# A state-space and gating mixer layer on one core: other buffers for the readout's tables, another split of the state copies, kernels between half blocks

## The chip, the core and the metric

The kernel runs on one NeuronCore of a Trainium2 chip. The metric is the device time of one execution in microseconds (us); the number for a version is the median over its runs. Engines are named as in the profile: PE is TensorE (PEld its weight loads), DVE is VectorE, ACT is ScalarE, POOL is GpSimd, SP is SyncE, whose queue issues every DMA of this kernel.

## What is computed

The reference is one layer over 1024 latent rows of width 1024 (float32). With `h` the layer-normed and modulated input and `p = h @ w_in + b_in` split into `ua, za, ub, vb, zb, ga, gb`:

```python
y_a, _ = _s5_bidir(ua, discs, ssm_c_re[i], ssm_c_im[i], ssm_d[i], ctx_final, True)
ya = _ssm_glu_gate(y_a, za, glu_w[i], glu_b[i])        # gelu(y), half-GLU, * silu(za)
yb = _sgu_branch(ub, vb, zb, ...)                      # gelu(ub) * (W_s v + b) * silu(zb)
out = _merge_out(ya, yb, ga, gb, w_branch_a[i], w_branch_b[i], w_out[i], b_out[i])
x = _layer_norm(DEEPNORM_ALPHA * x + gate[:, None] * out) * ln_g[i] + ln_b[i]
```

`_s5_bidir` is a diagonal linear recurrence over the positions, forward and backward, with 32 groups of 16 channels and 64 complex states a group; its output is read out of the states, with a direct term from the inputs. A context of 256 rows gives the recurrence its first state.

## The kernel before, in words

Tile builds the program: the code gives instructions in program order, each tile takes a free buffer of its pool, and a scheduler lays out, ahead of time and with its own estimate of durations, the order in which every engine's queue runs them; earlier lines have the higher priority. A queue runs strictly in the order it was given. Every large product is done as three float32r products (`mm3`, L75) of high and low halves; the halves of a weight are made on ACT (L72) and DVE (L73) from a staged copy.

**Pools** (L49 to L55): `G`, 27 buffers of 128x1024 float32; `WSP`, 6 of the same size, in which the high and low halves of the weights rotate as three pairs; `RAW`, 3, for the staged weights; `TMP`, 4 of 128x512; `ROW`, 2 of 128x1280; `BIG`, one, which holds the recurrence's states `vst` in the middle of the kernel. Sixteen of the `G` buffers hold the transposed `h` (`hth`, `htl`) until late.

**Recurrence in blocks of 8 positions.** `ua` is written to DRAM (`ud`) and read back in a block layout; `v_in` and `v_out` make the block inputs of all states; `scan` (L604) steps through the 158 blocks on DVE, three small operations a step. Steps 1 to 49 stand ahead of the other branch's projection, 50 to 158 beside it.

**Tables.** `out_powers(b)` (L625), for `b` 0 to 3 (8 groups each), makes on DVE two readout tables `kca` (six operations of 128x1024 for the two directions) and writes them to DRAM (`cad`). `kernels(b, d)` (L634) multiplies them on PE with `bbar` to the short convolution kernels inside a block, and writes these to DRAM (`wd`). These stand (L660 to L673) around two projection blocks, UB+2 and UB+3, each of which `proj` (L551) does as two half blocks of 512 rows, 24 products each; `mid` is called between the two halves.

**Branch B** (L829 to L839): eight times a projection of gate GB+i (48 products) and a product with `w_b` (24), `then_b` on DVE, and the result `mb` (a `G` buffer) to DRAM (`md`). The weights of block 27 (GB+7), `w_b3` and block 12 (the first of ZA) are split in this stage and hold the three pairs of `WSP` at its end.

**Readout** (L768 to L850). `y_tables(b)` loads from DRAM two tables `ca` (512 KB each; `G` for b = 0, `WSP` for the rest), a kernel table `mt` in eight pieces of 64 KB (`RAW`), and the rows of u, `um`, in two halves (`TMP`). `y_states(b)` (L781) copies the states from `vst` to two `G` tiles `z`, in eight copies of 64x512: four on ACT (L790), four on DVE (L792). `y_mm(b)` (L795) does 8 groups on PE, each one product with `mt` and `um` (L801) and two with `ca` and `z` (L803), and the gelu on ACT into `gk` (`ROW`). `y_trans(b)` (L808) transposes `gk` on PE (`pg`, L813) into `gT`. Program order on PE is y_mm 0, y_mm 1, trans 0, y_mm 2, trans 1, y_mm 3, trans 2, trans 3. In program order `y_tables(0)` and `y_states(0)` stand behind branch 6, `y_tables(1)` behind branch 7, and `y_states(b + 1)` and `y_tables(b + 2)` behind `y_mm(b)`.

After that come the projections ZA (`act_into`, L875), the GLU, branch A and the output product, on PE without a break until the tail.

Of the kernel before, what the change touches and what calls it, by code (L numbers as in the profile page):

```python
# [8 lines left out]
F32 = mybir.dt.float32  # L9
F32R = mybir.dt.float32r  # L10
I32 = mybir.dt.int32
AF = mybir.ActivationFunctionType
# [4 lines left out]
T = 8  # L17
# [9 lines left out]
UB, ZB, ZA, GA, GB = 0, 4, 8, 12, 20  # L27
# [8 lines left out]
def mixer_kernel(ctx: ExitStack, tc: tile.TileContext, a, out):  # L36
    nc = tc.nc
    V, S, Pl, PE = nc.vector, nc.scalar, nc.gpsimd, nc.tensor
# [5 lines left out]
    def pool_of(tag, bufs, dshape, ddt=F32):  # L44
        def make(name, shape=dshape, dt=ddt):
            return sb.tile(list(shape), dt, name=name, tag=tag, bufs=bufs)
        return make

    G = pool_of("g", 27, (128, 1024))  # L49
    BIG = pool_of("big", 1, (128, 2 * NSLOT * 32))  # L50
    RAW = pool_of("raw", 3, (128, 1024))
    WSP = pool_of("wsp", 6, (128, 1024), F32R)
    TMP = pool_of("tmp", 4, (128, 512))
    ROW = pool_of("row", 2, (128, 1280))
# [5 lines left out]
    def BANK(name, shape=(128, 512)):  # L60
        return psum.tile(list(shape), F32, name=name, tag="b", bufs=8)

    def dma(o, i):
        nc.sync.dma_start(o, i)
# [190 lines left out]
    ud = dram.tile([4, T, 128, 160], F32, name="ud")  # L255
# [200 lines left out]
    for j in range(2):  # L456
        t = RAW(f"xc{j}")
# [36 lines left out]
    for b in range(4):  # L494
        p = BANK(f"pcu{b}")
# [6 lines left out]
    def outer(dst, tmp, eng, pr, xr, xi, b, d, last):  # L502

        gs = slice(32 * d + 8 * b, 32 * d + 8 * b + 8)
        sh = [128, 8, 8, 16]

        def bc(i, x):
            return (pr[:, :, i, gs].rearrange("p k g -> p g k").unsqueeze(3).to_broadcast(sh),
                    x[:, gs, :].unsqueeze(2).to_broadcast(sh))
        p0, x0 = bc(0, xr)  # L510
        p1, x1 = bc(1, xi)
        eng.tensor_tensor(dst, p0, x0, op=OP.mult)
        eng.tensor_tensor(tmp, p1, x1, op=OP.mult)
        eng.tensor_tensor(dst, dst, tmp, op=last)
# [36 lines left out]
    def proj(blk, evac, ahead=None, mid=None):  # L551

        if ahead is None:
            ahead = 0 if blk == GB + 7 else 2
        wh, wl = weights(f"blk{blk}", ahead)
        for hf in range(2):
            p = BANK(f"pp{blk}{hf}")
            sl = slice(512 * hf, 512 * hf + 512)
            for k in range(8):
                mm3(p, wh[:, k, :], wl[:, k, :], hth[k][:, sl], htl[k][:, sl], k == 0, k == 7)  # L560
            evac(p, sl)
            if mid is not None and hf == 0:
                mid()

    def act_into(blk, fn, dst=None, then=None, ahead=None, mid=None):
        def evac(p, sl):
            t = dst[:, sl] if dst is not None else TMP("act")
            S.activation(t, p, fn, bias=cols[:, C_BLK + blk:C_BLK + blk + 1])
            if then is not None:
                then(t, sl)  # L570
        proj(blk, evac, ahead, mid)
# [4 lines left out]
    vm = [G("vm0")]  # L576
# [48 lines left out]
    def out_powers(b):  # L625
        for d in range(2):
            ca = G(f"kca{b}{d}", (128, 8, 8, 16))
            outer(ca, ROW("katmp", (128, 8, 8, 16)), V, pc, xcr, xci, b, d, OP.subtract)
            dma(cad[b, d], ca.rearrange("p g i h -> p (g i h)"))
            kca[b, d] = ca  # L630
# [3 lines left out]
    def kernels(b, d):  # L634
        if d == 0:
            pks[b] = BANK(f"pk{b}", (128, 2, 256))
        pk = pks[b]
        ca = kca[b, d]
        gg = 32 * d + 8 * b
        for k in range(4):  # L640
            for par in range(2):
                lh = bbar[:, gg + 2 * k:gg + 2 * k + 2, :].rearrange("p g h -> p (g h)")
                o = pk[32 * k:32 * k + 32, par, :]
                g = 2 * k + par
                PE.matmul(o[:, 128 * d:128 * d + 112], lh, ca[:, g, d:d + 7, :].rearrange("p i h -> p (i h)"),
                          start=True, stop=True)
                PE.matmul(o[:, 128 * d + 112:128 * d + 128], lh, xcr[:, gg + g, :], start=True, stop=True)
        if d == 0:
            return
        wk = TMP(f"wk{b}", (128, 2, 240))  # L650
        S.activation(wk[:, :, 0:112], pk[:, :, 128:240], AF.Copy)
        S.activation(wk[:, :, 128:240], pk[:, :, 0:112], AF.Copy)
        dm = TMP(f"dm{b}", (128, 3, 16))
        V.tensor_scalar(dm[:, 2, :], mask, cols[:, C_D + b:C_D + b + 1], None, op0=OP.mult)
        V.tensor_tensor(dm[:, 0:2, :], pk[:, :, 112:128], dm[:, 2, :].unsqueeze(1).to_broadcast([128, 2, 16]), op=OP.add)
        V.tensor_tensor(wk[:, :, 112:128], pk[:, :, 240:256], dm[:, 0:2, :], op=OP.add)
        for g in range(8):
            dma(wd[8 * b + g], wk[16 * g:16 * g + 16, g % 2, :])
# [2 lines left out]
        vm.append(G(f"vm{i}"))  # L661
    out_powers(0)
    out_powers(1)
    act_into(UB + 2, AF.Gelu_apprx_tanh, dst=vm[2])
    kernels(0, 0)
    kernels(0, 1)
    out_powers(2)
    kernels(1, 0)
    kernels(1, 1)
    out_powers(3)  # L670
    act_into(UB + 3, AF.Gelu_apprx_tanh, dst=vm[3], mid=lambda: (kernels(2, 0), kernels(2, 1)))
    kernels(3, 0)
    kernels(3, 1)  # L673

    scan(1, 50)

# [65 lines left out]
    for i in range(2, 4):  # L742
        def then(t, sl):
            V.tensor_tensor(vm[i][:, sl], vm[i][:, sl], t, op=OP.mult)
# [3 lines left out]
    def branch(i, g0, w, y, then):  # L748

        banks = []  # L750

        def evac(p, sl):
            t = TMP("act")
            S.activation(t, p, AF.Sigmoid, bias=cols[:, C_BLK + g0 + i:C_BLK + g0 + i + 1])  # L754
            banks.append((t, sl))
        proj(g0 + i, evac)
        wh, wl = weights(f"{w}{i // 2}")
        cs_ = slice(128 * (i % 2), 128 * (i % 2) + 128)
        for t, sl in banks:
            p = BANK(f"pb{g0 + i}")  # L760
            for k in range(4):
                mm3(p, wh[:, k, cs_], wl[:, k, cs_], y[k][0][:, sl], y[k][1][:, sl], k == 0, k == 3)
            then(t, p, sl)


    cas, mts, ums, zs, gks, gt = {}, {}, {}, {}, {}, []

    def y_tables(b):  # L768
        for d in range(2):
            ca = (G if b == 0 else WSP)(f"ca{b}{d}", (128, 8, 8, 16), F32)  # L770
            dma(ca.rearrange("p g i h -> p (g i h)"), cad[b, d])
            cas[b, d] = ca
        mts[b] = RAW(f"mt{b}", (128, 8, 128))
        for s in range(8):
            dma(mts[b][16 * s:16 * s + 16],
                wd[8 * b:8 * b + 8, :, 16 * (7 - s):16 * (7 - s) + 128].rearrange("g h w -> h g w"))
        ums[b] = [TMP(f"um{b}{h}", (128, 4, 128)) for h in range(2)]
        for h in range(2):
            dma(ums[b][h], ud[b].rearrange("t (h g) c -> (t h) g c", g=8)[:, 4 * h:4 * h + 4, 32:160])

    def y_states(b):  # L781
        for d in range(2):
            zt = G(f"z{b}{d}", (128, 8, 128))
            o = 31 if d == 0 else 33
            for cp in range(2):
                for par in range(2):
                    dst = zt[64 * cp:64 * cp + 64, par:8:2, :]
                    src = vst[64 * par:64 * par + 64, d, o:o + 128, cp, 4 * b:4 * b + 4].rearrange("p c q -> p q c")
                    if par == 0:
                        S.activation(dst, src, AF.Copy)  # L790
                    else:
                        V.tensor_copy(dst, src)  # L792
            zs[b, d] = zt

    def y_mm(b):  # L795
        gks[b] = ROW(f"gk{b}", (128, T, 128))
        for h in range(2):
            p = BANK(f"py{b}{h}", (128, 4, 128))
            for i in range(4):
                g = 4 * h + i  # L800
                PE.matmul(p[:, i, :], ums[b][h][:, i, :], mts[b][:, g, :], start=True, stop=False)  # L801
                for d in range(2):
                    PE.matmul(p[:, i, :], zs[b, d][:, g, :], cas[b, d][:, g].rearrange("p i h -> p (i h)"),  # L803
                              start=False, stop=d == 1)
            S.activation(gks[b][:, :, 64 * h:64 * h + 64].rearrange("p t (g h) -> p g t h", h=16),
                         p.rearrange("p g (t h) -> p g t h", h=16), AF.Gelu_apprx_tanh)
# [23 lines left out]
    for i in range(8):  # L830
        mb = G(f"mb{i}")

        def then_b(t, p, sl):
            V.tensor_tensor(mb[:, sl], t, p, op=OP.mult)
        branch(i, GB, "w_b", yb, then_b)
        dma(md[i], mb)
        if i == 6:
            y_tables(0)
            y_states(0)  # L839

    y_tables(1)
    for b in range(4):
# [44 lines left out]
    for i in range(8):  # L887
# [16 lines left out]
        if i == 4:  # L904
# [3 lines left out]
            for h in range(2):  # L908
                p = BANK(f"pga{h}")
# [141 lines left out]
```

## Time and profile before

| | |
|---|---|
| median of 3 runs (742.08 to 742.7) | 742.08 us |
| the profiled execution | 743.85 us |
| its span, first to last instruction | 742.1 us |
| mean granted TensorE clock | 0.992 |
| PE busy | 710.3 us, 96% |
| DVE, ACT, POOL busy | 465.1, 244.5, 38.5 us |
| readout on PE, from the first `py` product to the first ZA product | 415.84 to 449.00 us |

The profile is one execution. Its span leaves out 1.75 us around the instructions that the execution's own time has. PE's clock is given as a share of the higher of its two levels (2.4 GHz), so 0.5 is the lower (1.2 GHz). Idle time of an engine is listed with what ended it; idle time of an engine that does not hold up the others costs nothing.

### The profile page before, as it was taken

Reading aid. Unit: us, or ns where it says so; the run is one execution under the profiler, and the core shown is the slowest. Engines: PE = TensorE matmul, PEld = TensorE weight load, DVE = VectorE, ACT = ScalarE, POOL = GpSimd, SP = SyncE. Lnnn points to the kernel's source line nnn. Section 1 sums busy time; section 2 is a strip of 40 time slices with the busy share of each in tenths; the row PEclk is TensorE's granted clock in tenths of the full one; section 3 lists DMA queues with packets and bytes.
Section 4 is the critical chain, followed back from the end, with each engine's and each line's share of the span. In section 5 each row is a group of like instructions: output and inputs, shape, how many; then the busy total and the mean of one; then the engine's idle time right before and its main releaser. Section 6 shows DMA issues by size and latency. Waiting matters only on the chain.

```text
span 742.1 us, 10068 instructions
## 1 busy us (share of the span) xinstructions
PE 710.3 (96%) x3924; PEld 587.5 (79%) x3924; DVE 465.1 (63%) x1059; ACT 244.5 (33%) x348; POOL 38.5 (5%) x41
## 2 busy tenths in 40 slices
PE   3889999999999999999999979999999999999995
PEld 1656798887888888888888968888888878888885
DVE  4487963569789585899995535134543334592995
ACT  3357737751105423111121865135111211350000
POOL 1010133000001000000000000000000000000221
PEclk9999999999999999999999999999999999999998
DMA  7950273624411211121216674111353223151441
GB/s 301 346 211 30 57 207 114 192 86 150 134 57 30 76 45 52 57 86 57 85 61 193 189 211 150 50 57 57 133 179 114 86 87 112 58 187 40 157 144 69
DMA packets 40783, 87.27 MB, mean 118 GB/s; under 512 B 8352, under 2 KB 21280, under 8 KB 40736
## 3 DMA queue, kind: packets, MB, share of 16 engines
q1 hardware_dynamic: 40736, 86.63, 34.9%
q8 instruction: 31, 0.51, 0.3%
q14 instruction: 16, 0.13, 0.1%
HBM read 70.92 MB, written 15.70 MB: 117 GB/s over the span
## 4 chain that ended last, share of the span: by engine, by line
PE 87%; DVE 5%; ACT 3%; DMA 2%; issue 1%; SPq 0%; POOL 0%; DVEq 0%; ACTq 0%; POOLq 0%
PE pp L77 13%; PE pp L78 13%; PE pp L79 13%; PE po L947 4%; PE po L946 4%; PE po L945 4%; PE pb L78 4%; PE pb L79 4%; PE pb L77 4%; PE pvb L690 2%; PE pvb L691 2%; PE pvb L692 2%; PE pv L546 2%; PE py L803 2%; PE pu L77 1%; PE pm L206 1%
## 5 line engine op out<-in xcount | busy, mean ns | idle before, releaser
L77 PE MATMUL pp<-hh,h_blk 128*128 128x512 f32 x448 | 175.5, 392 | 0.0
L79 PE MATMUL pp<-hl,h_blk 128*128 128x512 f32 x448 | 174.6, 390 | 0.0
L78 PE MATMUL pp<-hh,l_blk 128*128 128x512 f32 x448 | 174.4, 389 | 0.0
L77 PEld LDWEIGHTS pp<-hh,h_blk 128*128 128x128 f32 x448 | 84.1, 188 | 18.4 <-issue 0.6
L79 PEld LDWEIGHTS pp<-hl,h_blk 128*128 128x128 f32 x448 | 84.1, 188 | 17.5
L78 PEld LDWEIGHTS pp<-hh,l_blk 128*128 128x128 f32 x448 | 84.1, 188 | 17.4 <-DVE m L894 0.2
L73 DVE TENSOR_TENSOR l_blk<-r_blk,h_blk 128x1024 fp32r<-128x1024 f32 x28 | 34.9, 1247 | 50.6 <-ACT h_blk L72 49.8
L72 ACT ACTIVATE h_blk<-r_blk 128x1024 fp32r<-128x1024 f32 x28 | 29.9, 1069 | 98.0 <-PE pp L78 49.6
L754 ACT ACTIVATE act<-pp,cols 128x512 f32<-128x512 f32 x32 | 21.8, 682 | 96.9 <-PE pp L79 73.2
L608 DVE TENSOR_TENSOR scm<-acat,vst 128x128 f32<-128x128 f32 x158 | 46.0, 291 | 9.8 <-ACT vst L548 5.0
L612 DVE TENSOR_TENSOR vst<-vst,scs 128x64 f32<-128x64 f32 x158 | 35.4, 224 | 4.8
L611 DVE TENSOR_TENSOR scs<-scm 128x64 f32<-128x64 f32 x158 | 35.4, 224 | 4.6
L945 PE MATMUL po<-wobig,mh 128*128 128x512 f32 (+1 forms) x90 | 32.9, 365 | 0.0
L946 PE MATMUL po<-wobig,mh 128*128 128x512 f32 (+1 forms) x90 | 32.9, 365 | 0.0
L947 PE MATMUL po<-wobig,ml 128*128 128x512 f32 (+1 forms) x90 | 32.9, 365 | 0.0
L77 PE MATMUL pu<-hh,uw 128*128 128x512 f32 x64 | 27.4, 433 | 2.5 <-ACT uw L72 1.9
L79 PE MATMUL pu<-hl,uw 128*128 128x512 f32 x64 | 26.5, 417 | 0.9 <-DVE hl L200 0.9
L78 PE MATMUL pu<-hh,uw 128*128 128x512 f32 x64 | 26.5, 414 | 0.0
L690 PE MATMUL pvb<-h_vb,hh 128*128 128x512 f32 x64 | 25.1, 393 | 0.0
L691 PE MATMUL pvb<-l_vb,hh 128*128 128x512 f32 x64 | 24.9, 389 | 0.0
L79 PE MATMUL pb<-yas,h_w_a 128*128 128x512 f32 x64 | 24.9, 389 | 0.0
L79 PE MATMUL pb<-ybl,h_w_b 128*128 128x512 f32 x64 | 24.9, 389 | 0.0
(341 smaller groups left out, 1332.0 us busy)
## 6 DMA issues: line engine op xcount, KB each, us to landing
r_blk<-in_w_blk SPq DMA_DIRECT2D x28, 512.0 KB, 3.4
wm<-in_wm SPq DMA_DIRECT2D x16, 512.0 KB, 7.3
x<-in_x SPq DMA_DIRECT2D x8, 512.0 KB, 6.7
cad<-kca SPq DMA_DIRECT2D x8, 512.0 KB, 2.9
md<-mb SPq DMA_DIRECT2D x8, 512.0 KB, 2.7
ca<-cad SPq DMA_DIRECT2D x8, 512.0 KB, 5.8
mb<-md SPq DMA_DIRECT2D x8, 512.0 KB, 4.5
wgt<-in_w_gate SPq DMA_DIRECT2D x8, 512.0 KB, 3.3
```

Of the source, the lines that this page charges most:

```text
L73: return first, (eng or V).tensor_tensor(lo, src, hi.bitcast(F32), op=OP.subtract)
L77: PE.matmul(o, wh, rh, start=first, stop=False)
L78: PE.matmul(o, wl, rh, start=False, stop=False)
L79: PE.matmul(o, wh, rl, start=False, stop=last)
L608: V.tensor_tensor(scm, acat.rearrange("p d (o c) q -> p d o (c q)", o=2), both(n - 1, prev).unsqueeze(2).to_broadcast([128, 2, 2, 32]), op ...
L611: V.tensor_tensor(scs4, m4[:, :, 0, :], m4[:, :, 1, :], op=OP.add)
L612: V.tensor_tensor(both(n, 160 if n == 31 else cur), both(n, cur), scs2, op=OP.add)
L690: PE.matmul(pvb[kk], hth[k][:, ks], wh[:, j, :], start=k == 0, stop=False)
L691: PE.matmul(pvb[kk], hth[k][:, ks], wl[:, j, :], start=False, stop=False)
L945: PE.matmul(p, mh, wh, start=k == 0, stop=False)
L946: PE.matmul(p, mh, wl, start=False, stop=False)
L947: PE.matmul(p, ml, wh, start=False, stop=k == 7)
```

## The change

Four things. Around UB+2 and UB+3 the kernels of each `b` stand between or behind the half blocks: half of UB+2, kernels 0 and `out_powers(2)`, half of UB+2, kernels 1 and `out_powers(3)`, half of UB+3, kernels 2, half of UB+3, kernels 3. The tables `ca` of b = 0 take `WSP` buffers like the others, `um` is one `ROW` tile loaded by one DMA, and `gk` takes `G` buffers. Of the eight state copies of a `b`, two stay on ACT and six are on DVE. `y_states(0)` stands one branch earlier, behind branch 5.

```diff
--- before.py
+++ after.py
@@ -661,16 +661,17 @@
         vm.append(G(f"vm{i}"))
     out_powers(0)
     out_powers(1)
-    act_into(UB + 2, AF.Gelu_apprx_tanh, dst=vm[2])
-    kernels(0, 0)
-    kernels(0, 1)
-    out_powers(2)
-    kernels(1, 0)
-    kernels(1, 1)
-    out_powers(3)
-    act_into(UB + 3, AF.Gelu_apprx_tanh, dst=vm[3], mid=lambda: (kernels(2, 0), kernels(2, 1)))
-    kernels(3, 0)
-    kernels(3, 1)
+
+    def kernel_step(b):
+        kernels(b, 0)
+        kernels(b, 1)
+        if b < 2:
+            out_powers(b + 2)
+
+    act_into(UB + 2, AF.Gelu_apprx_tanh, dst=vm[2], mid=lambda: kernel_step(0))
+    kernel_step(1)
+    act_into(UB + 3, AF.Gelu_apprx_tanh, dst=vm[3], mid=lambda: kernel_step(2))
+    kernel_step(3)
 
     scan(1, 50)
 
@@ -767,16 +768,15 @@
 
     def y_tables(b):
         for d in range(2):
-            ca = (G if b == 0 else WSP)(f"ca{b}{d}", (128, 8, 8, 16), F32)
+            ca = WSP(f"ca{b}{d}", (128, 8, 8, 16), F32)
             dma(ca.rearrange("p g i h -> p (g i h)"), cad[b, d])
             cas[b, d] = ca
         mts[b] = RAW(f"mt{b}", (128, 8, 128))
         for s in range(8):
             dma(mts[b][16 * s:16 * s + 16],
                 wd[8 * b:8 * b + 8, :, 16 * (7 - s):16 * (7 - s) + 128].rearrange("g h w -> h g w"))
-        ums[b] = [TMP(f"um{b}{h}", (128, 4, 128)) for h in range(2)]
-        for h in range(2):
-            dma(ums[b][h], ud[b].rearrange("t (h g) c -> (t h) g c", g=8)[:, 4 * h:4 * h + 4, 32:160])
+        ums[b] = ROW(f"um{b}", (128, 8, 128))
+        dma(ums[b], ud[b].rearrange("t (h g) c -> (t h) g c", g=8)[:, :, 32:160])
 
     def y_states(b):
         for d in range(2):
@@ -786,19 +786,19 @@
                 for par in range(2):
                     dst = zt[64 * cp:64 * cp + 64, par:8:2, :]
                     src = vst[64 * par:64 * par + 64, d, o:o + 128, cp, 4 * b:4 * b + 4].rearrange("p c q -> p q c")
-                    if par == 0:
+                    if par == 0 and cp == 0:
                         S.activation(dst, src, AF.Copy)
                     else:
                         V.tensor_copy(dst, src)
             zs[b, d] = zt
 
     def y_mm(b):
-        gks[b] = ROW(f"gk{b}", (128, T, 128))
+        gks[b] = G(f"gk{b}", (128, T, 128))
         for h in range(2):
             p = BANK(f"py{b}{h}", (128, 4, 128))
             for i in range(4):
                 g = 4 * h + i
-                PE.matmul(p[:, i, :], ums[b][h][:, i, :], mts[b][:, g, :], start=True, stop=False)
+                PE.matmul(p[:, i, :], ums[b][:, g, :], mts[b][:, g, :], start=True, stop=False)
                 for d in range(2):
                     PE.matmul(p[:, i, :], zs[b, d][:, g, :], cas[b, d][:, g].rearrange("p i h -> p (i h)"),
                               start=False, stop=d == 1)
@@ -834,9 +834,10 @@
             V.tensor_tensor(mb[:, sl], t, p, op=OP.mult)
         branch(i, GB, "w_b", yb, then_b)
         dma(md[i], mb)
+        if i == 5:
+            y_states(0)
         if i == 6:
             y_tables(0)
-            y_states(0)
 
     y_tables(1)
     for b in range(4):
```

## Rows read from the trace of the kernel before

**Rows 1.** The page, part 1: busy time, share of the span, instructions.

```profile
PE 710.3 (96%) x3924; PEld 587.5 (79%) x3924; DVE 465.1 (63%) x1059; ACT 244.5 (33%) x348; POOL 38.5 (5%) x41
```

**Rows 2.** TensorE's waits over the whole span: total us, times, longest.

```profile
PE pt L223 <- ACT x L189: 11.2, 2, 11.0
```

**Rows 3.** TensorE in order of time: start, us, operation, idle before in brackets.

```profile
415.84 0.38 PE L801 MATMUL py<-mt,um 128*128 128x128 f32 x2
...
421.20 0.39 PE L801 MATMUL py<-mt,um 128*128 128x128 f32 x2
...
427.55 1.09 PE L813 MATMUL pg<-ident,gk 128*128 128x128 f32 x8 [0.83 <-ACT gk L805]
431.72 0.46 PE L801 MATMUL py<-mt,um 128*128 128x128 f32 x2 [3.08 <-DMA um<-ud]
...
441.14 0.46 PE L801 MATMUL py<-mt,um 128*128 128x128 f32 x2 [1.33 <-issue]
...
448.15 1.09 PE L813 MATMUL pg<-ident,gk 128*128 128x128 f32 x8 [0.54 <-ACT gk L805]
449.00 0.48 PE L77 MATMUL pp<-hh,h_blk 128*128 128x512 f32 x1
```

**Rows 4.** Stretch: us; busy PE, PEld, DVE, ACT, POOL; granted clock; DMA share, GB/s.

```profile
432.00:436.00 4.00, 4.00 (x24) 4.00 (x23) 1.23 (x1) 2.61 (x3) 0.00 (x0) 0.58 0.97 291
```

**Rows 5.** SyncE's queue in order of time: start, us of issuing, transfer.

```profile
400.86 4.04 SPq L64 DMA_DIRECT2D mt<-wd  x6
410.36 0.81 SPq L64 DMA_DIRECT2D ca<-cad  x2
411.23 0.42 SPq L64 DMA_DIRECT2D mt<-wd  x1
415.93 0.37 SPq L64 DMA_DIRECT2D um<-ud  x1
...
419.61 1.38 SPq L64 DMA_DIRECT2D ca<-cad  x2
421.04 6.18 SPq L64 DMA_DIRECT2D mt<-wd  x8
427.46 2.20 SPq L64 DMA_DIRECT2D um<-ud  x2
429.75 0.93 SPq L64 DMA_DIRECT2D ca<-cad  x2
430.74 7.00 SPq L64 DMA_DIRECT2D mt<-wd  x8
437.78 0.98 SPq L64 DMA_DIRECT2D um<-ud  x2
```

**Rows 6.** SyncE's wait ended within 410 to 411 us.

```profile
SPq L64 <- PE pp L79: 4.6, 1, 4.6
```

**Rows 7.** Transfers issued within 410 to 411 us: count, KB each, us to landing.

```profile
ca<-cad SPq DMA_DIRECT2D x2, 512.0 KB, 4.2
```

**Rows 8.** Transfers issued within 427 to 428.5 us, the same columns.

```profile
um<-ud SPq DMA_DIRECT2D x2, 256.0 KB, 4.2
```

**Rows 9.** Tile ca, landing times of its eight transfers.

```profile
DMA to landing us min/median/max: 3.5/5.8/7.5
```

**Rows 10.** ScalarE's groups within 407 to 426 us: busy, mean ns, idle before.

```profile
L790 ACT ACTIVATE z<-vst 64x512 f32<-64x512 f32 x12 | 13.5, 1128 | 14.2 <-DMA md<-mb 11.6 <-PE pb L78 2.4
```

**Rows 11.** VectorE's groups within 399 to 432 us, the same columns.

```profile
L792 DVE COPY z<-vst 64x512 f32<-64x512 f32 x16 | 10.7, 670 | 12.2 <-DMA md<-mb 6.8 <-PE pb L78 5.1
```

**Rows 12.** VectorE in order of time: the first two kca tables; state copies behind branch 7.

```profile
162.09 2.35 DVE L514 TENSOR_TENSOR kca<-kca,katmp 128x1024 f32<-128x1024 f32 x2
...
413.77 1.42 DVE L792 COPY z<-vst 64x512 f32<-64x512 f32 x2 [5.11 <-PE pb L78]
```

**Rows 13.** TensorE: end of a half block of UB+2, and the kernels' wait.

```profile
159.81 0.39 PE L79 MATMUL pp<-hl,h_blk 128*128 128x512 f32 x1
...
169.13 0.35 PE L645 MATMUL pk<-kca,bbar 128*32 128x112 f32 x2 [0.91 <-DVE kca L514]
```

## The prediction

> **What bounds the kernel now.** I read the page first, then TensorE's waits, then TensorE and SyncE in order of time through the readout. PE is busy for 710.3 of 742.1 us [rows 1], so all that a change of order or of buffers can win lies in the 31.8 us between. The largest wait, 11.2 us for the first rows of x, is at the start [rows 2], where nothing changes. What the change touches is the readout: its first product starts at 415.84, right behind branch 7 with no idle time ahead of it, and the first ZA product at 449.00, 33.2 us later [rows 3]. One y_mm takes 421.20 - 415.84 = 5.36 us. A transposition, eight products, is 1.09 us. Four of each are 25.8 us, so the stage loses 7.4. Four waits are in it [rows 3]: 0.83 of y_trans(0) for a gelu, 3.08 of y_mm(2) for um2, 1.33 of y_mm(3), put down to issue, and 0.54 of y_trans(3). The rest is the clock: from 432 to 436 us PE is granted 0.58 [rows 4], mostly the lower of its two levels, after a stretch in which it had little more than the transposition to do; 4 x 0.42 = 1.7 us. With the 5.8 of the waits that is the loss.
>
> Why is um2 late? In SyncE's queue um2 is issued at 427.46, behind two ca2 transfers and eight pieces of mt2 that took 6.18 us to issue, and um3 at 437.78, behind 7.00 us for mt3 [rows 5]. y_mm(3) starts 3.36 us after the issue of um3 began, so I read its "issue" as the landing of um3. From 419.61 to 438.76 the queue has no pause. **The readout's second half is bounded by that queue**, and its end is y_mm(3)'s start plus the 449.00 - 441.14 = 7.86 us that follow.
>
> **Part by part.**
>
> *State copies.* ACT's twelve copies up to 426 us cost 13.5 us, 1128 ns each; DVE's sixteen 670 ns each [rows 10, 11]. With two and six, a b costs ACT 2.3 and DVE 4.0 us, both under y_mm's 5.36. ACT then has four copies for b = 1 and 2 in place of eight, and reaches the first gelu about 4.5 us earlier, so the 0.83 us wait goes. DVE is loaded instead: z of b = 1 can start when branch 7 frees its buffers, at 413.77 [rows 12], and its six copies end near 417.8, ahead of y_mm(1) at 421.20. The cover is 3.4 us, less two products for mb that run between.
>
> *States one branch earlier.* ACT stood 11.6 us waiting for the write of mb to free a buffer [rows 10]. That goes, but y_mm(0) did not wait for z, so it is worth nothing on the path. mb 7 then has to wait for the buffer of mb 6, but is first written at the end of branch 7.
>
> *um in ROW, gk in G.* um0 and um1 find both ROW buffers free, so um1 leaves SyncE's queue ahead of 410 us; before, its first half was issued at 415.93 [rows 5]. Two issues become one. gk finds the G buffers that branch 7 frees: nothing. A whole um can land later than the half on which y_mm waited; 0 to 0.5 us, I take 0, because the half's wait was for the queue.
>
> *ca0 in WSP.* This is the price. The pairs hold w_b3, block 27 and block 12, so ca0 takes block 27's, freed at 410.36, where before ca1 was issued after 4.6 us of waiting [rows 5, 6]. Those two transfers landed 4.2 us after issue [rows 7], the second at 415.0; the first use comes just behind 415.84, so I take no wait. By the slowest landing of a table, 7.5 us [rows 9], it would be 2.3 us late. ca1 takes w_b3's pair, free at 415.9, and lands at about 415.9 + 0.4 + 4.2 = 420.5, also just in time. ca2 now waits for y_mm(0), ca3 for y_mm(1).
>
> *The queue after 421.3.* When y_mm(0) ends, ca2, um2 and mt3 get their buffers; mt2 has had the third RAW buffer all along. With k pieces of mt2 still to be issued, um3's issue starts at 421.3 + 0.93 (ca2) + 0.77k (6.18 / 8) + 1.0 (um2) + 7.00 (mt3) + 0.93 (ca3), and y_mm(3) starts 3.36 later: 434.5 + 0.77k. PE without waits would be there at 421.20 + 2 x (5.36 + 1.09) = 434.1, so the queue decides. For k = 0 this is 434.5 and a gain of 6.6 us, for k = 4 it is 437.6 and 3.5 us, for k = 8 it is 440.7 and 0.4 us. What speaks for a small k: before, six pieces of mt1 in a row went ahead of ca1 while it waited for its pair [rows 5]. What speaks for a large one: the last piece went behind it, though the queue stood still for 4.6 us [rows 6], and none of mt2 went ahead of ca2. The queue is laid out by a planner whose clock the trace does not show, so I take the middle, **k = 4**. Then um2 lands at 425.3 + 4.2 = 429.5 [rows 8], y_mm(2) waits 2 us instead of 3.08, and even 1.7 us of the lower clock would be over before um3 lands.
>
> *Kernels between half blocks.* PE's work is the same. The one wait there is 0.91 us for kca of b = 1 [rows 13]. Best case: it goes. Worst case: kernels 0 hold PE between the halves. The first half of UB+2 ends at 160.1 [rows 13], the first two tables at 164.44 [rows 12]: 4.4 us of waiting, 3.5 more than now. I take 0: PE's order already puts other products in where kernels are not ready, and would keep the second half in front.
>
> **Sum.** 441.14 - 437.6 = 3.5 us off the profiled execution's 743.85; its smaller waits lie within that. The runs' median, 742.08, is 1.8 below that execution, so I forecast 742.08 - 3.5 = **738.6 us**.
>
> **Rivals.**
>
> *All of mt2 goes ahead.* y_mm(3) starts at 434.5, or PE fills the waits with ZA products; with the 0.91 us of the kernels the gain is 6.6 to 7.5 us: 734.6 to 735.5. For it: from 404.90 to 419.61 the queue spends under 3 us on issues [rows 5], time enough for eight pieces. Chance 0.26.
>
> *No change.* k is 6 to 8, or a wait of the kernels eats the gain: 741 to 743. The buffers then moved nothing in the queue's order, and the change does not do what it says. Chance 0.20.
>
> *Slower: tables at the head of the queue.* A transfer that waits for its buffer holds every transfer behind it, as ca1 held mt1's last piece until 411.23 [rows 5]. If ca2 stands ahead of all of mt2, nothing of mt2, um2, mt3 moves before 421.3. With the prices that issues had under load [rows 5], 421.3 + 1.38 + 6.18 + 2.20 + 0.93 + 7.00 + 3.36 = 442.4, and up to 1 us more if ca0 or the whole um lands late: 1.3 to 2.3 us lost, 743.4 to 744.4. It decides from k = 7 at these prices. Chance 0.16.
>
> The Trainium skill, "DMA: Bandwidth & Descriptors", section "Anatomy of one DMA", states that the DMA engines don't wait on semaphores and that any such wait happens on the issuing sequencer before dispatch. The wait and the held piece agree [rows 5, 6]; by this rule alone, every buffer that ties a table to a later event is a loss, and the slower rival's time would be the forecast.
>
> **How the numbers follow.** The forecast has 0.38, from k of 2 to 5. A change under 0.2%, about 1.5 us, can't be told from none here. Faster gets the forecast and the first rival, 0.64; same 0.20; slower 0.16. The range runs from the best case with the kernels' wait gone, 734.8, to the slower rival's middle, 743.9; the forecast's own range is 737 to 740.
>
> **What would show it.** In the changed profile: y_trans(0) with no wait; um2 issued before 426 and y_mm(3) at 437 to 438; the clock between 427 and 441 higher than 0.58; ca0 issued at about 410.4 and no wait at the first `ca` product. Wrong for the forecast would be pieces of mt2 behind ca2 (the last two rivals), a wait at 416 for ca0, a wait of kernels 0 above 2 us near 160, or ZA products between the y_mm of the readout (the first rival).

## The result and the profile after

The changed kernel took **749.12 us**, median of 4 runs (748.45 to 749.93), beside 742.08 for the kernel before: a ratio of 1.0094, interval 1.0076 to 1.0111. I had forecast 738.6 and a range of 734.8 to 743.9; the sign was wrong and the range missed. In a later series (run e5 below) the same code came out at 1.0041, interval 1.0020 to 1.0062. Slower it is both times; by how much differs by more than the intervals, and the section on the experiments says what of that is understood.

The profiled execution took 748.45 us, with a span of 746.5 against 742.1. First the page of the changed kernel, part 1, and of TensorE's waits the rows that changed (total us, times, longest):

```profile
PE 714.7 (96%) x3924; PEld 591.1 (79%) x3924; DVE 470.3 (63%) x1067; ACT 234.7 (31%) x340; POOL 39.2 (5%) x41
```

```profile
PE pk L645 <- DVE kca L514: 3.3, 1, 3.3
PE py L801 <- DMA ca<-cad: 3.2, 1, 3.2
...
PE pg L813 <- ACT gk L805: 0.5, 1, 0.5
```

PE has as many products as before, but is "busy" for 4.4 us more [rows 1]. A product counts as busy for longer when its clock is lower (two `py` products in a row take 0.39 us at full clock and 0.77 in the row at 436.62 below), so this row already says that clock was lost. The wait on `kca` was 0.9 us [rows 13]; it is now the second longest of the whole span.

Cutting both spans at the same instructions shows where the 4.4 us came in. From the last `pv` product (of `v_out`, L546) to the first `ps` product (the gating branch, L725), the stretch that holds UB+2, UB+3 and the kernels: 102.1 us before, 106.7 after. The readout: 33.2 before, 32.0 after. Everything between those two stretches and behind them agrees within 0.1 us. The start-up ahead of the last `pv` product was 1.0 us longer in this execution, on the same instructions: 4.6 - 1.2 + 1.0 = 4.4.

**The kernels.** TensorE of the changed kernel in order of time (start, us, operation, idle before), and the stretches around it (the columns of rows 4, the granted clock third from the end):

```profile
160.82 0.39 PE L79 MATMUL pp<-hl,h_blk 128*128 128x512 f32 x1
164.47 0.35 PE L645 MATMUL pk<-kca,bbar 128*32 128x112 f32 x2 [3.26 <-DVE kca L514]
```

```profile
160.00:164.00 4.00, 1.21 (x6) 0.67 (x4) 4.00 (x4) 0.00 (x0) 0.00 (x0) 1.00 0.00 0
164.00:168.00 4.00, 3.53 (x45) 2.87 (x46) 4.00 (x5) 0.00 (x0) 0.00 (x0) 0.74 0.66 257
168.00:172.00 4.00, 4.00 (x37) 3.51 (x34) 4.00 (x5) 1.30 (x3) 0.00 (x0) 0.83 0.33 131
172.00:176.00 4.00, 4.00 (x43) 3.25 (x42) 4.00 (x7) 1.34 (x2) 0.00 (x0) 1.00 0.40 152
```

The first half of UB+2 ends at 161.2, and what stands next in PE's queue is kernels 0, not the second half. PE stands still for 3.26 us, and behind the stall it is granted 0.74 and 0.83 for 4 us each: 4 x (0.26 + 0.17) = 1.7 us more. Why is `kca` late? VectorE and ScalarE of the changed kernel in order of time:

```profile
157.24 0.29 DVE L608 TENSOR_TENSOR scm<-acat,vst 128x128 f32<-128x128 f32 x1 [4.95 <-ACT vst L548]
...
158.56 2.35 DVE L512 TENSOR_TENSOR kca<-pwf,xc 128x1024 f32<-128x1024 f32 x2
160.83 2.36 DVE L513 TENSOR_TENSOR katmp<-pwf,yc 128x1024 f32<-128x1024 f32 x2
163.10 2.36 DVE L514 TENSOR_TENSOR kca<-kca,katmp 128x1024 f32<-128x1024 f32 x2
```

```profile
152.46 4.75 ACT L548 ACTIVATE vst<-pv 128x320 f32<-128x320 f32 x8
157.23 1.06 ACT L617 ACTIVATE xc<-xc 64x1024 f32<-64x1024 f32 x1
```

VectorE sits idle for 4.95 us although the first table's products need nothing of the scan: the first scan step stands ahead of them in its queue and waits for eight copies of `vst` on ScalarE. The sign change of `xc`, an input of the tables, stands behind the same eight copies. The first table is done at 164.3 and the second at 165.5. Before, the same late tables were covered by the second half of UB+2.

**The readout.** SyncE's queue, TensorE and the stretches of the changed kernel, in the columns of rows 5, 3 and 4:

```profile
416.01 0.81 SPq L64 DMA_DIRECT2D ca<-cad  x2
416.88 0.42 SPq L64 DMA_DIRECT2D mt<-wd  x1
421.45 0.32 SPq L64 DMA_DIRECT2D ca<-cad  x1
422.47 0.32 SPq L64 DMA_DIRECT2D md<-mb  x1
422.88 4.72 SPq L64 DMA_DIRECT2D ca<-cad  x3
427.66 2.32 SPq L64 DMA_DIRECT2D mt<-wd  x5
430.02 0.53 SPq L64 DMA_DIRECT2D um<-ud  x1
433.24 0.82 SPq L64 DMA_DIRECT2D ca<-cad  x2
434.11 5.52 SPq L64 DMA_DIRECT2D mt<-wd  x8
439.85 0.53 SPq L64 DMA_DIRECT2D um<-ud  x1
```

```profile
427.74 1.05 PE L813 MATMUL pg<-ident,gk 128*128 128x128 f32 x8
428.70 0.49 PE L803 MATMUL py<-ca,z 128*128 128x128 f32 x2
...
436.62 0.77 PE L801 MATMUL py<-mt,um 128*128 128x128 f32 x2 [3.19 <-DMA ca<-cad]
...
445.68 0.39 PE L801 MATMUL py<-mt,um 128*128 128x128 f32 x2
...
452.61 1.10 PE L813 MATMUL pg<-ident,gk 128*128 128x128 f32 x8 [0.54 <-ACT gk L805]
```

```profile
433.50:437.50 4.00, 0.88 (x4) 0.91 (x5) 1.99 (x4) 1.70 (x3) 0.00 (x0) 0.76 1.08 335
437.50:441.50 4.00, 4.00 (x21) 4.00 (x21) 0.00 (x0) 0.00 (x0) 0.00 (x0) 0.50 0.93 162
441.50:445.50 4.00, 4.00 (x34) 4.00 (x34) 0.00 (x0) 3.35 (x4) 0.00 (x0) 0.89 0.88 254
```

The first product starts at 421.49. The waits in the stage fell from 5.8 us [rows 3] to 3.19 + 0.54 = 3.7: y_trans(0) no longer waits, nor does y_mm(3). But the clock cost more. It had fallen before y_mm(2) began, so in the first of the three stretches only the 0.88 us of work count, all of it at 0.50: 0.88 x 0.50 + 4 x (0.50 + 0.11) = 2.9 us, against 1.7 before [rows 4]. Of 2.1 us won in waits, 1.2 went back to the clock. The row of the 3.19 us names `ca`; but the pair of block 2 had landed at 432.8, and what landed last ahead of y_mm(2) was um2, at 436.2. The queue did what the change was for: `ca` of block 2 is held until y_mm(0) ends, with five pieces of `mt2` and um2 behind it. From 429.5 to 437.5 the 16 DMA engines are fully busy (1.09 and 1.08).

### The profile page after: what moved, and what is told of

Read it like the earlier page. It is cut to its first block, busy times and chain, and to the rows that moved or that the text cites. A ratio compares the mean times of both kernels' runs of the same rounds, so it can differ in the third digit from the quotient of the medians.

```text
span 746.5 us, 10064 instructions
## 1 busy us (share of the span) xinstructions
PE 714.7 (96%) x3924; PEld 591.1 (79%) x3924; DVE 470.3 (63%) x1067; ACT 234.7 (31%) x340; POOL 39.2 (5%) x41
## 4 chain that ended last, share of the span: by engine, by line
PE 90%; DVE 4%; ACT 3%; DMA 1%; issue 1%; POOL 0%; SPq 0%; DVEq 0%; POOLq 0%
PE pp L77 14%; PE pp L78 13%; PE pp L79 13%; PE po L948 4%; PE po L946 4%; PE po L947 4%; PE pb L79 4%; PE pb L78 4%; PE pb L77 4%; PE py L803 2%; PE pvb L692 2%; PE pvb L691 2%; PE pvb L693 2%; PE pv L546 2%; PE pu L77 1%; PE pk L645 1%
## 5 line engine op out<-in xcount | busy, mean ns | idle before, releaser
L77 PEld LDWEIGHTS pp<-hh,h_blk 128*128 128x128 f32 x448 | 84.2, 188 | 18.4 <-issue 0.6
L755 ACT ACTIVATE act<-pp,cols 128x512 f32<-128x512 f32 x32 | 21.8, 682 | 100.1 <-PE pp L79 76.4
L946 PE MATMUL po<-wobig,mh 128*128 128x512 f32 (+1 forms) x90 | 32.9, 365 | 0.0
L947 PE MATMUL po<-wobig,mh 128*128 128x512 f32 (+1 forms) x90 | 32.9, 365 | 0.0
L948 PE MATMUL po<-wobig,ml 128*128 128x512 f32 (+1 forms) x90 | 32.9, 365 | 0.0
L693 PE MATMUL pvb<-h_vb,hl 128*128 128x512 f32 x64 | 24.9, 389 | 0.0
```

The lines of the kernel that those rows point to most:

```text
L77: PE.matmul(o, wh, rh, start=first, stop=False)
L693: PE.matmul(pvb[kk], htl[k][:, ks], wh[:, j, :], start=False, stop=k == 7)
L946: PE.matmul(p, mh, wh, start=k == 0, stop=False)
L947: PE.matmul(p, mh, wl, start=False, stop=False)
L948: PE.matmul(p, ml, wh, start=False, stop=k == 7)
```

## The experiments

Theory A: the loss is the order around UB+2, because PE reaches kernels 0 before `kca` is ready. Theory B, my own rival: the loss is the held queue of the readout. Twelve runs, in three series; each ratio is to the kernel before in the same series. "Kernels" is the stretch from the last `pv` to the first `ps` product, "readout" the stage as above, "clock loss" is counted as above, for the time in which TensorE was at work. The last five columns come from one profile each; two profiles of one kernel (before and e0, after and e5) differ by 0.3 and 0.4 us in the readout.

| run | median, us | ratio, interval | kernels | wait on kca | readout | its waits | its clock loss |
|---|---|---|---|---|---|---|---|
| before (first profile) | 742.08 | | 102.1 | 0.9 | 33.2 | 5.8 | 1.7 |
| after (first profile) | 749.12 | 1.0094, 1.0076 to 1.0111 | 106.7 | 3.3 | 32.0 | 3.7 | 2.9 |
| e0 before again | 743.03 | 0.9996, 0.9971 to 1.0021 | 102.0 | 0.9 | 32.9 | 5.5 | 1.7 |
| e1 readout only | 742.13 | 0.9978, 0.9955 to 1.0001 | 102.0 | 0.9 | 31.4 | 4.1 | 1.7 |
| e2 kernels only | 749.06 | 1.0076, 1.0051 to 1.0100 | 106.6 | 3.3 | 32.6 | 6.8 | 0 |
| e3 sign on VectorE | 746.77 | 1.0049, 1.0030 to 1.0067 | 106.5 | 4.3 | 33.0 | 4.9 | 2.7 |
| e4 scan behind tables | 741.72 | 0.9962, 0.9941 to 0.9983 | | | | | |
| e5 change again | 746.22 | 1.0041, 1.0020 to 1.0062 | 106.7 | 3.3 | 32.4 | 4.6 | 2.5 |
| e6 mt one block ahead | 742.45 | 0.9986, 0.9965 to 1.0008 | 102.1 | 0.9 | 31.2 | 5.4 | 0 |
| e7 um, gk and copies only | 741.38 | 0.9967, 0.9948 to 0.9986 | 102.0 | 0.9 | 30.0 | 4.5 | 0 |
| e8 e4 with readout of e7 | 740.34 | 0.9967, 0.9944 to 0.9990 | 100.8 | 0 | 32.4 | 5.1 | 1.7 |
| e9 e4, one run | 741.99 | | 100.8 | 0 | 32.6 | 4.2 | 3.0 |
| e10 readout, ca0 in G | 744.29 | 1.0017, 0.9993 to 1.0041 | 102.1 | 0.9 | 34.3 | 6.0 | 2.4 |
| e11 e7, scan behind tables | 739.18 | 0.9969, 0.9945 to 0.9992 | 100.8 | 0 | 29.8 | 4.3 | 0 |

In the profiled execution of e4, which lasted 4036.74 us, the 128x512 products took about 1.7 us in place of 0.39 (one execution of e7 lasted 1443.97 us), so its rows are left out, and e9 is the same kernel with a usual profile.

### The parts of the change by themselves

e0 is the kernel before. e1 is the changed kernel with the order around UB+2 put back, e2 the kernel before with that order alone:

```diff
     # e1, from after (e2 is the reverse edit, from before)
-    act_into(UB + 2, AF.Gelu_apprx_tanh, dst=vm[2], mid=lambda: kernel_step(0))
-    kernel_step(1)
...
+    act_into(UB + 2, AF.Gelu_apprx_tanh, dst=vm[2])
+    kernels(0, 0)
+    kernels(0, 1)
...
```

> The kernel before, unchanged, for a second profile: 742.1 us within 0.2%, TensorE's wait for kca near 169 about 0.9 us, the readout from 415 to 449 us with about 7 us of waits and low clock. If the second profile's waits differ by over 1 us from the first's, differences of that size between two profiles mean nothing.

> The change with its kernels and half blocks put back as before, so only the readout's buffers and copies are new. Theory A (the loss is TensorE's wait for the first kca tables between the half blocks, with the low clock behind it): 740 to 742 us, about 1 us under the kernel before, no wait near 160 over 1 us. Theory B (the loss is the tables in the weight pairs, late at the head of SyncE's queue): 746 to 749 us.

> The kernel before with only the new order of kernels and half blocks. Theory A: 746 to 750 us, with the wait of about 3.3 us for kca near 161 us and a granted clock under 0.9 in the 8 us behind it. Theory B: 741 to 743 us.

The order alone is the whole loss: the kernels' stretch is 106.6 us with it and 102.0 without, and the ratio is 1.0076 with it and 0.9978 without. Theory B falls: with the held queue and the old order the kernel is not slower than before. The two parts add to 1.0054, between the two measurements of the whole, 1.0094 and 1.0041 (e5, below the 1.005 to 1.010 that I expected). What makes those two differ I did not settle; one known source is the start-up, which put the last `pv` product anywhere from 151.8 to 157.3 us in these profiles. It stood at 155.2 in the changed kernel's first profile and at 152.8 in e5, and their spans differ by about as much, 746.5 and 744.4 us.

### Making kca early

e3 moves the sign change off ScalarE, where it stood behind the `vst` copies:

```diff
-    S.activation(xcr[64:128], xcr[64:128], AF.Copy, scale=-1.0)
+    V.tensor_scalar(xcr[64:128], xcr[64:128], -1.0, None, op0=OP.mult)
```

> The whole change, with the sign change of the c tables (one operation of 64x1024 that kca's first product needs) on VectorE instead of ScalarE, where it stands behind eight copies of states. Theory A, with its cause named (kca starts at 158.6 us because that operation runs at 157.2): kca starts near 150 us, the wait for kca near 161 us goes, and the time falls by 4 to 8 us to 741 to 745. Theory B: no change against the changed kernel, 748 to 750 us.

A miss. The wait grew to 4.3 us and the stretch stayed at 106.5. VectorE of e3 in order of time:

```profile
155.84 0.29 DVE L608 TENSOR_TENSOR scm<-acat,vst 128x128 f32<-128x128 f32 x1 [4.95 <-ACT vst L548]
156.17 0.69 DVE L617 TENSOR_SCALAR xc<-xc 64x1024 f32<-64x1024 f32 x1
...
157.03 3.49 DVE L512 TENSOR_TENSOR kca<-pwf,xc 128x1024 f32<-128x1024 f32 x3
```

The sign change is now on VectorE, but behind the same scan step with its same 4.95 us. I had taken away one of two things in front of the tables, and the other was enough. So e4 keeps that edit and has the scan wait, in the planner's order, for the last operation of the first tables (`out_powers` keeps its instruction in `kl`):

```diff
-    scan(1, 50)
+    with tc.issue_after(kl[0].ins):
+        scan(1, 50)
```

> The changed kernel with two edits: the sign change of xcr is on VectorE, and the scan is told to wait in the planner's order until the last operation of out_powers(0), so that VectorE takes the first table's products before its first scan step. Theory A (the loss is the 3.3 us for which TensorE waits on kca, and the clock that falls behind it, because scan steps and vst copies stand ahead of kca on VectorE and ScalarE): kca starts near 149 to 151 us instead of 158.6, is done by 157, the wait near 161 us goes and the granted clock stays at 1.00; from the last product of the pv half blocks to the first of the next stage 101 to 102.5 us instead of 106.7, and the whole 4 to 5 us below the changed kernel, 0.993 to 0.999 of the kernel before. Rival C (the kernels' own products between the half blocks cost it, whatever kca does): the wait goes but the stretch stays near 106 us, ratio 1.004 to 1.010. Rival D: the delayed scan becomes the next wait (pt or pv behind vst), the stretch is above 104 us.

> The changed kernel once more, as a control in the same series. Same kernel, so 1.005 to 1.010 of the kernel before; the stretch with the kernels 106.7 us and the readout 31.9 us as in its first profile, with the wait of 3.3 us on kca and the one of 3.2 us at the products of block 2. If the ratio comes out nearer 1.005, the sum of the two part runs (1.0076 and 0.9978) holds without an interaction.

> The kernel of e4 once more for its profile, since in the profiled execution of e4 every product took several times its usual time. Theory A: kca done before 158 us, no wait on it above 0.5 us, stretch of the kernels 100.5 to 102.5 us against 106.6 in the changed kernel; readout 31.5 to 32.5 us.

VectorE and TensorE of e9, in order of time:

```profile
149.88 1.23 DVE L73 TENSOR_TENSOR l_vb<-r_vb,h_vb 128x1024 fp32r<-128x1024 f32 x1 [10.35 <-PE pA L537]
151.14 0.69 DVE L617 TENSOR_SCALAR xc<-xc 64x1024 f32<-64x1024 f32 x1
151.87 3.50 DVE L512 TENSOR_TENSOR kca<-pwf,xc 128x1024 f32<-128x1024 f32 x3
155.28 2.35 DVE L513 TENSOR_TENSOR katmp<-pwf,yc 128x1024 f32<-128x1024 f32 x2
157.55 2.35 DVE L514 TENSOR_TENSOR kca<-kca,katmp 128x1024 f32<-128x1024 f32 x2
```

```profile
159.64 0.39 PE L79 MATMUL pp<-hl,h_blk 128*128 128x512 f32 x1
159.96 0.38 PE L646 MATMUL pk<-kca,bbar 128*32 128x112 f32 x2
```

The idle 4.95 us are gone, the tables are done at 159.9, just as the first half block ends, and the kernels follow with no wait. They came some 2 us later than I expected, since VectorE put a third table's product in between, but still in time. The stretch falls by 5.9 us, to 100.8, and in the same series e4 stands at 0.9962 where the change stands at 1.0041. Theory A is confirmed by taking its cause away. Of the 5.9 us, 3.26 are the wait and 1.7 the clock; about 1 us more lies in neither row. It goes with the place of the later kernels: in the changed kernel three and four projection products stand between the two kernels of b = 1 and of b = 2, which in e3 and e9 run without a break (64 products from 168.74 to 171.33 us in e9), and e3's stretch less its wait and its clock is 106.5 - 4.3 - 1.7 = 100.5 us, near e9's.

### The readout

The readout improved less than I had forecast, so three runs change it alone, on the old order of the kernels. e6 issues `mt` one block ahead, which takes the five pieces of `mt2` out from behind the held `ca2`. e7 leaves `ca` of block 0 and the place of `y_states(0)` as they were. e10 is e1 with `ca` of block 0 in `G`:

```diff
     # e6, from e1: in y_tables(b), behind ca and um
-        mts[b] = RAW(f"mt{b}", (128, 8, 128))
+        for c in (0, 1) if b == 0 else (b + 1,) if b < 3 else ():
+            mts[c] = RAW(f"mt{c}", (128, 8, 128))
...
     # e10, from e1 (e7 has y_states(0) at i == 6 besides)
-            ca = WSP(f"ca{b}{d}", (128, 8, 8, 16), F32)
+            ca = (G if b == 0 else WSP)(f"ca{b}{d}", (128, 8, 8, 16), F32)
```

> The kernel of the readout alone (kernels stage as before), with the pieces of mt emitted one block ahead and um ahead of them: SyncE's five last pieces of mt2 now stand ahead of ca2, which waits for the products of block 0, and behind that wait only ca2, um2 and mt3 are left. Theory E (the 3.2 us wait at the products of block 2 is there because mt2's five pieces and um2 are held behind ca2's wait in the queue): um2 is issued 2 to 3 us after ca2 instead of 7 us, the wait of 3.2 us falls below 0.5 us and the readout takes 28 to 29 us instead of 31.4; ratio 0.992 to 0.996. Theory F (the transfers are short of DMA bandwidth, so the order of issue does not matter): the wait stays at 2 to 3.5 us, on another tile, and the readout stays at 31 to 32 us; ratio 0.996 to 0.999.

> The kernel before with only the buffers of um and gk exchanged and six of the eight state copies on VectorE; the tables of block 0 stay in the buffers of before and the states of block 0 in their place. Theory G (the gain of the readout comes from the shorter queue: one transfer of um for two, and no gk wait): readout 31 to 32 us as in the run of the readout alone, ratio 0.996 to 0.999. Theory H (it comes from the tables of block 0, which start earlier): readout stays at 32.6 to 33.2, ratio 0.999 to 1.001.

> The readout of the change with only the tables of block 0 put back into the buffers of before (kernels stage as before). Theory J (the tables of block 0 in the weight pairs cost the readout time, because then ca2 has no pair left that is free and waits for the products of block 0 with mt2 and um2 behind it): ca2 is issued without a wait of microseconds, mt2's rest is issued by the end of the products of block 0, and the readout is 29.5 to 30.5 us as in e7, ratio 0.995 to 0.998. Rival K (e7's 30.0 us came from another source, such as the states' place or the spread between executions): readout 31 to 32 us as in e1.

e6: theory E falls. The order of issue moved as meant and um2 was issued 2.3 us behind `ca2`, but it took 7.5 us to land, in a stretch where the DMA share was 1.10 and 1.14; y_mm(2) still waited 2.86 us, and y_mm(3) 1.6. e7 did better than either theory: 30.0 us. e10 went to 34.3, outside both. The table shows what they have in common: readout less waits less clock loss is 25.3 to 25.8 us in every run. The spread is waits and clock. In e7 two waits stand at full clock; TensorE and one stretch of e7:

```profile
428.41 0.46 PE L800 MATMUL py<-mt,um 128*128 128x128 f32 x2 [2.12 <-DMA ca<-cad]
...
436.71 0.46 PE L800 MATMUL py<-mt,um 128*128 128x128 f32 x2 [1.83 <-DMA um<-ud]
```

```profile
426.50:430.50 4.00, 2.09 (x19) 2.12 (x20) 3.93 (x6) 0.53 (x1) 0.00 (x0) 1.00 1.03 307
```

In e10 the wait is a single one at um3, and the clock falls behind it; TensorE and the stretches of e10:

```profile
439.31 0.77 PE L800 MATMUL py<-mt,um 128*128 128x128 f32 x2 [5.03 <-DMA um<-ud]
```

```profile
435.20:439.20 4.00, 0.00 (x0) 0.00 (x0) 2.71 (x3) 1.78 (x2) 0.00 (x0) 0.77 0.84 248
439.20:443.20 4.00, 3.89 (x18) 3.92 (x19) 1.23 (x1) 1.06 (x1) 0.00 (x0) 0.50 0.76 294
443.20:447.20 4.00, 4.00 (x34) 4.00 (x33) 0.00 (x0) 0.77 (x2) 0.00 (x0) 0.88 0.42 131
```

In e10 `ca3`, which waits for the end of y_mm(1), was issued 12.2 us behind the first product, in e7 10.7; `mt3` and um3 stand behind it in the queue. In e10 five of the products of y_trans(0) stand inside y_mm(1), as all eight do in the changed kernel (427.74, above; `ca3` at 11.8); in e7 they stand behind it. The state copies say why. ScalarE of the changed kernel:

```profile
427.54 1.11 ACT L790 ACTIVATE z<-vst 64x512 f32<-64x512 f32 x1
```

This is the last copy that y_mm(1) needs. It ends at 428.65, 7.2 us behind the first product, and the next `ca` product starts at 428.70; y_trans(0) fills the time. In e10 it ends 7.6 us behind the first product, and TensorE waits the last 0.21 us for it. In e7 that copy ends 5.5 us behind the first product. So the earlier states, which e10 and the changed kernel have and e7 has not, also hold back the release that um3 waits for. This part repeats: `ca3` left 11.8 us behind the first product in each of the five profiles with the change's readout (after, e1, e3, e5, e9) and 10.7 in the three with e7's (e7, e8, e11). The stage as a whole does not: the readout of e7 took 30.0, 32.4 and 29.9 us in those three, so of the 4.3 us between e7 and e10 only the 1.5 us at `ca3` are shown to be the states' doing.

### Putting the parts together

e8 is e4 with the readout of e7; e11 is e7 with the edits of e3 and e4, so the order of before with early tables.

> The kernels' order of the change with the scan behind the first table (as in e4) and the readout of e7 (tables of block 0 in the buffers of before). Theory A: the stretch from the last pv product to the first ps product takes 100.5 to 102 us and TensorE has no wait on kca above 0.5 us, with the granted clock at 1.00 through the stage; readout 30.0 us as in e7; together 4 to 6 us below the kernel before, ratio 0.992 to 0.995. Rival C: the stretch stays above 104 us though no wait on kca is left, ratio 0.999 to 1.003.

> The readout of e7 with the kernels' order of before, and the scan behind the first table. It tells whether the order of the change is worth anything by itself once kca comes early. If the order is worth nothing (my own step in the prediction): the stretch is the same as in e8 within 0.5 us, near 101.2 us (102.1 less the 0.9 us wait on kca), and the ratio the same as e8's within its interval. If products between half blocks gain by themselves: 1 us or more above e8.

With early tables the new order takes 100.8 us and the old one 100.8: the order itself is worth nothing. The ratios agree too, 0.9967 and 0.9969, a little short of what I expected of e8, whose readout was 32.4 and not 30.0 us. SyncE's queue in e8 has the same transfers in the same order as in e11; what differs is the wait at y_mm(3), 3.2 us against 2.5, and the clock behind it. e11 has the lowest median, 739.18 us, about 0.3% below the kernel before, and the changed kernel stands at 1.0041 in e5. But e4 (0.9962), e7 (0.9967), e8 and e11 can't be told apart by their intervals; that early tables are worth 1.3 us on the old order is seen in the stretch (102.0 in e7, 100.8 in e11) and not in the ratios.

## Why the prediction was wrong

**Kernels between half blocks: the step that failed.** The prediction had the right rows and the right worst case, "4.4 us of waiting, 3.5 more than now", and then took 0, because "PE's order already puts other products in where kernels are not ready, and would keep the second half in front". It did not. PE takes its queue in the order laid out beforehand, and kernels 0 were laid out ahead of the second half; the planner's estimate probably has `kca` ready earlier than the chip has, but no trace shows that estimate. That the old order held no long wait was no evidence that the planner avoids one: there, the second half of UB+2 stood in front because the code said so. The wait came at 3.26 us, 2.35 more than before, and the worst case was itself too small, since it left out the clock behind a stall (1.7 us). In all the step cost 4.6 us, and no rival held that: "no change" has a wait of the kernels that eats the gain, and no more, and the slower case was priced on the readout alone.

**State copies: right in their outcome, by luck in their times.** The 0.83 us wait of y_trans(0) is gone; y_mm(1) follows y_mm(0) without one. But the copies for block 1 on VectorE were to end 3.4 us ahead of y_mm(1); they began only at 422.5 and ended at 426.6, 0.3 us ahead of it, and the second one on ScalarE ended 1.8 us behind its start, under y_trans(0). That the earlier states are "worth nothing on the path" missed their price: y_trans(0) inside y_mm(1) delays `ca3`, `mt3` and um3 by about 1 us.

**um in ROW, gk in G: no wait of their own**, as said. But "a whole um can land later than the half", for which I took 0, was worth more: um2 landed 6.1 us after its issue, where the halves had 4.2 [rows 8] (4.9 in e7, where the 16 engines were less busy).

**ca0 in WSP: right.** It is issued as block 27's pair comes free, 5.5 us ahead of the first product as forecast, and the first `ca` product has no wait, with 0.6 us to spare.

**The queue: the right number by luck, the wrong price, and wrong in what it bounds.** With k = 4, um3 was to be issued 18.4 us behind the first product of the readout (437.6 - 3.36 - 415.84); it was, at 439.85 - 421.49 = 18.36, with five pieces held. But the terms differ. The sum has 12.9 us of issues between y_mm(0) and um3; in the changed kernel `ca2`, five pieces, um2, `ca3` and `mt3` take 10.3 us of queue, and the other 2.7 are a wait for the end of y_mm(1), from 430.55 to 433.24, which the sum has not. In e3, e5 and e9, with the same readout, um3 left at 20.1, 19.6 and 19.2. The price was misread from a row: "the queue has no pause" from 419.61 to 438.76 is not so. SyncE's waits of the kernel before in 419 to 439 us, in the columns of rows 6:

```profile
SPq L64 <- DMA ca<-cad: 6.1, 4, 3.2
```

Of the 6.18 us for `mt2` and the 7.00 for `mt3`, 6.1 in all were waits for a `ca` to land, not issuing; five pieces without such a wait took 2.32 us. In every profile of the table but e6, which has another order, um3 left within 0.6 us of the landing of the second `ca3`. So um3 hangs on that landing, and through it on the end of y_mm(1).

The Trainium skill, "DMA: Bandwidth & Descriptors", section "Anatomy of one DMA", says that any wait of a DMA for a semaphore happens on the issuing sequencer, ahead of the dispatch. The 4.72 us row with `mt2` and um2 behind it agrees. The slower case did not come true even so: three pieces of `mt2` had gone ahead, and the other five cost 2.32 us. (Pieces behind `ca2` were on the prediction's list of what would prove it wrong, though its own k = 4 has them.)

What also failed is that y_mm(3) no longer waited for um3. It started 24.2 us behind the first product, not 21.8, because y_mm(2) waited 3.19 us and not 2, and then ran from 436.62 to 445.68, 9.06 us with its transposition, in place of 6.45. "Even 1.7 us of the lower clock would be over before um3 lands" was mis-sized: it was 2.9, and um3, which landed at 444.6, was no longer the last to come. So the readout gave 1.2 us in place of 3.5 (1.7 in e1, 0.7 in e5).

**The rivals.** "Tables at the head of the queue" had the sign, but not the size, and the wrong mechanism; e1, which keeps the held queue, is not slower. The prediction had listed "a wait of kernels 0 above 2 us near 160" among what would prove the forecast wrong. It is the row that did, but it should have had a chance and a price of its own. The range's lower end, 734.8, also lies above the first rival's own best case, 742.08 - 7.5 = 734.6.

## What to carry to other kernels

Where work is moved ahead of a cover, price the new place by when its inputs are ready in the trace, not by what the planner did elsewhere: here the inputs' end (164.4) and the new place's start (160.1) both stood in the rows, and their difference, 4.3 us, was nearer to the measured 3.26 than the 0 that I took. A stall of the matrix engine is to be priced with the clock that can fall behind it. And a late input can be mended on another engine's queue: with the sign change and the scan moved on VectorE, both orders of the products took 100.8 us, and nothing was left between them.

## What the runs showed of the hardware that I had not expected

The clock behind a wait does not follow from the length of that wait alone: in the readout it fell behind one of 2.36 us (e0, 0.94 and 0.63 in the two stretches) and stayed at 1.00 through one of 2.86 (e6) and one of 3.69 (e2). Where it fell in the readout it cost 1.7 us, or 2.4 to 3.0, about half as much as the wait or more. So two kernels with the same order of transfers, e8 and e11, differ by 2.5 us in one stage of their profiles, 1.7 of it clock, and a gain in waits of 1 to 2 us can be lost or doubled. I did not test what decides it.

The transfers of the readout take longer when more of them are sent early: 512 KB of um2 took 4.9 us to land in e7, at a DMA share of 0.86 to 1.03, 6.1 in the changed kernel at 1.09, and 7.5 in e6. In e6, where the queue was freed for um2, the wait only moved: the 16 engines were full.

SyncE's queue never had more than eight transfers between issue and landing, in any of the fourteen profiles. With eight out, the next one left as the oldest landed: in e6 the second table of block 1 landed at 425.81 us and um2 left at 425.82; in the changed kernel the seventh piece of `mt3` left 0.02 us behind the first `ca3`, the last piece 0.02 us behind the second. So what reads as slow issuing under load is in part slow landing. Whether the chip or the program sets the eight, no run shows.
